# A masked prefix sum gathered at the midpoint: SyncE and TensorE loop over pairs of batches

## The chip, the core and the metric

The kernel runs on one core of one Trainium2 chip. The metric is the device time of one execution in microseconds (us), the median of several runs. The profile's times are in us from the start of the profiled span.

The engines that matter here: TensorE (PE in the profile; its weight loads are PEld, its sequencer PEq), VectorE (DVE), ScalarE (ACT), GpSimd (POOL) and SyncE (SP). Each runs its own list of instructions; they meet only at semaphores. SP and ACT also issue transfers, which 16 DMA engines carry out, and a transfer that has landed adds 16 to its semaphore.

## The reference

```
def reference(x, lengths, w):
    B, S, D = x.shape                      # 8, 8192, 512
    pos = np.arange(S)[None, :, None]
    mask = (pos < lengths[:, None, None]).astype(np.float32)
    masked = x * mask
    cs = np.cumsum(masked, axis=1)
    midpoints = (lengths // 2).clip(0)
    b_idx = np.arange(B)
    mid_features = cs[b_idx, midpoints, :]
    return np.matmul(mid_features[:, None, :], w).squeeze(1).astype(np.float32)
```

For each batch this is the sum of the first n = min(length // 2 + 1, length) rows of x, times w. Only those rows have to be read. The inputs are the same in every run; the eight values of n are 570, 2690, 256, 2057, 905, 3772, 3859 and 571. In blocks of 512 rows (1 MB) that is 1, 5, 0, 4, 1, 7, 7 and 1 whole blocks, 26 in all, and remainders of 58, 130, 256, 9, 393, 188, 275 and 59 rows.

## The kernel before

The sums are matrix products: a block of 512 rows lies as four rows in each of 128 partitions (G = 4), and TensorE multiplies it from the left by a matrix of 128 x 8 whose column b is one and whose other columns are zero (`sel`, shifted by b). The four rows of a partition go to four column groups of the array (`tile_position`), and all products of all batches are added up in one PSUM tile, `s_ps`. One matmul of the program is two matmul and two weight-load instructions in the profile, so a block is 8 of each.

The code is written out for all eight batches, and each batch has code for up to NB = 8 blocks, behind a branch for each block: `whole_blocks` (L107) goes on while n is at least 512 (k + 1).

SP (L118 to L182) first issues the load of the lengths, `lens1` (L120), which takes every other 32-bit word. `Counts` (L86) waits for it, loads the eight lengths into registers (L95), and works out n when a batch is first asked for (L101: three register operations, one fused instruction). Then come all blocks of all batches, in order (L135). Batch b writes to half b % 2 of `xt`, place k. Before it may, `wait_free` (L124) waits until TensorE has consumed what was there: `s_free[c]` counts the blocks of batch c that are done, and the newest earlier batch of the same half that has a block k is searched by branches (L127). Behind all blocks come the remainders of all batches (L147 to L178), each into a place of its own in `rem`: for each of 256, 128 and 64 one transfer if that bit of n is set (L152), and one for up to 64 last rows (L164). GpSimd clears the eight places of `rem` first, 14.1 us of work (L199). At the end SP issues half of the output (L182).

ACT issues the load of `w` (L187, 1 MB) and of a copy of the lengths for all partitions, `lens` (L188), at the start, and the other half of the output at the end.

VectorE makes `sel`, then the `mask` that says which of a remainder's places hold rows that count, in a chain of small steps (L210 is the helper that records each), among them `fold`, `cnt` and `cap`. Last it copies `s_ps`, `mf_ps` and `o_ps` out of PSUM, each when TensorE is done with it.

TensorE clears `s_ps` with eight products of zeros (L267), loads its own copy of the counts, goes through the blocks of all batches (L273 to L279; the matmul's line is that of the helper, L261), then waits for the mask and goes through the eight remainders (L282 to L286). Then it folds the four column groups into one and transposes in one product (L291), and multiplies by w (L298).

What sets the order of the work: SP's one list (all blocks, then all remainders), and TensorE's (the same). Everything else is beside it.

Of the kernel before, what the change touches and what calls it, by code (L numbers as in the profile page):

```python
# [8 lines left out]
I32 = mybir.dt.int32  # L9
ALU = mybir.AluOpType  # L10
ds = bass.ds
P = 128
# [3 lines left out]
def kernel(  # L16
# [22 lines left out]
    PARTS = [(256, 0, 2), (128, 1, 4), (64, 3, 8)]  # L39
    LAST = (7, 8)  # L40
    xf = x.rearrange("b s d -> (b s) d")
# [4 lines left out]
    def sb(name, shape, dt=F32):  # L46
        return ctx.enter_context(nc.sbuf_tensor(name, shape, dt))
# [4 lines left out]
    def sem(name):  # L52
        return tc.alloc_semaphore(name)

    xt = sb("xt", [P, 2, NB, G, D])
    rem = sb("rem", [P, B, G, D])
    wt = sb("wt", [P, KC, D])
    lens1 = sb("lens1", [1, B], I32)
# [8 lines left out]
    mask = sb("mask", [P, B * (G * B + 1)])  # L67
    sel = sb("sel", [P, 2 * B - 1])
# [11 lines left out]
    s_full = [[sem(f"full{b}_{k}") for k in range(NB)] for b in range(B)]  # L80
    s_rem = [sem(f"rem{b}") for b in range(B)]
    s_free = [sem(f"free{b}") for b in range(B)]
    s_w, s_len, s_len1, s_out = sem("w"), sem("len"), sem("len1"), sem("out")
    s_pool, s_dve, s_pe = sem("pool"), sem("dve"), sem("pe")

    class Counts:  # L86


        def __init__(self, eng):
            self.eng = eng  # L90
            self.regs = [eng.alloc_register(f"n_{eng.engine.name}_{b}") for b in range(B)]
            self.t = eng.alloc_register(f"t_{eng.engine.name}")
            self.known = 0
            eng.wait_ge(s_len1, 16)
            eng.load(self.regs, lens1[:])  # L95

        def __getitem__(self, b):
            while self.known <= b:

                n = self.regs[self.known]  # L100
                self.eng.reg_alu(self.t, n, 1, ALU.logical_shift_right)  # L101
                self.eng.reg_alu(self.t, self.t, 1, ALU.add)
                self.eng.reg_alu(n, self.t, n, ALU.min)
                self.known += 1
            return self.regs[b]

    def whole_blocks(eng, n, body, k=0):  # L107
        if k < NB:
            with eng.If_cmp(n, BLK * (k + 1), "IS_GE"):  # L109
                body(k)  # L110
                whole_blocks(eng, n, body, k + 1)

    POOL_REM = 1 + B
    DVE_SEL, DVE_MASK = 3, 28
# [3 lines left out]
    @block.sync  # L118
    def _(sp):
        sp.dma_start(out=lens1[:], in_=lens_words[:, ::2]).then_inc(s_len1, 16)  # L120
        ns = Counts(sp)
        t = ns.t

        def wait_free(b, k):  # L124

            if b >= 0:
                with sp.If_cmp(ns[b], BLK * (k + 1), "IS_GE"):  # L127
                    sp.wait_ge(s_free[b], k + 1)
                with sp.Else():
                    wait_free(b - 2, k)  # L130

        for b in range(B):
            def load_block(k):
                wait_free(b - 2, k)
                sp.dma_start(  # L135
                    out=xt[:, b % 2, k],
                    in_=x[b, k * BLK:(k + 1) * BLK].rearrange("(p g) d -> p g d", g=G),
                ).then_inc(s_full[b][k], 16)

            whole_blocks(sp, ns[b], load_block)  # L140

        def rows(b, first, count):
            return xf[ds(sp.snap(first) + b * S, count)]

        sp.wait_ge(s_pool, POOL_REM)
        base = sp.alloc_register("base")
        for b in range(B):  # L147
            for count, first, step in PARTS:
                sp.reg_alu(t, ns[b], count, ALU.bitwise_and)
                with sp.If_cmp(t, 1, "IS_GE"):  # L150
                    sp.reg_alu(base, ns[b], ~(2 * count - 1), ALU.bitwise_and)
                    sp.dma_start(  # L152
                        out=rem[first::step, b],
                        in_=rows(b, base, count).rearrange("(p g) d -> p g d", g=G),
                    ).then_inc(s_rem[b], 16)
                with sp.Else():
                    sp.sem_inc(s_rem[b], 16)
            sp.reg_alu(t, ns[b], 63, ALU.bitwise_and)
            sp.reg_alu(base, ns[b], ~63, ALU.bitwise_and)

            def load_last(lo, hi):

                if hi - lo == 1:
                    sp.dma_start(  # L164
                        out=rem[LAST[0]::LAST[1], b, :hi],
                        in_=rows(b, base, 16 * hi).rearrange("(g p) d -> p g d", p=16),
                    ).then_inc(s_rem[b], 16)
                    return
                mid = (lo + hi) // 2
                with sp.If_cmp(t, 16 * mid, "IS_GT"):  # L170
                    load_last(mid, hi)
                with sp.Else():
                    load_last(lo, mid)

            with sp.If_cmp(t, 1, "IS_GE"):
                load_last(0, 4)
            with sp.Else():
                sp.sem_inc(s_rem[b], 16)  # L178

        sp.wait_ge(s_dve, DVE_MASK + 3)  # L180
        for j in range(0, 4, 2):
            sp.dma_start(out=out[:, j * P:(j + 1) * P], in_=o_sb[32 * j:32 * j + B]).then_inc(s_out, 16)  # L182
        sp.wait_ge(s_out, 64)

    @block.scalar
    def _(act):
        act.dma_start(out=wt[:], in_=w.rearrange("(kc p) d -> p kc d", p=P)).then_inc(s_w, 16)  # L187
        act.dma_start(out=lens[:], in_=lens_words.to_broadcast((P, 2 * B))).then_inc(s_len, 16)  # L188
        act.wait_ge(s_dve, DVE_MASK + 3)
        for j in range(1, 4, 2):  # L190
            act.dma_start(out=out[:, j * P:(j + 1) * P], in_=o_sb[32 * j:32 * j + B]).then_inc(s_out, 16)

    @block.gpsimd
    def _(pool):
        pool.iota(pid[:], pattern=[[0, 1]], base=0, channel_multiplier=1)
        pool.iota(thr_i[:], pattern=[[128, G]], base=0, channel_multiplier=1)
        pool.iota(fold_i[:], pattern=[[-1, B]], base=128, channel_multiplier=1).then_inc(s_pool, 1)
        for b in range(B):
            pool.memset(rem[:, b], 0.0).then_inc(s_pool, 1)  # L199

    @block.vector
    def _(dve):
        done = 0

        def step(do, *args, **kw):

            nonlocal done
            if done:
                dve.wait_ge(s_dve, done)
            do(*args, **kw).then_inc(s_dve, 1)  # L210
            done += 1

        step(dve.memset, zero[:], 0.0)
        step(dve.memset, sel[:], 0.0)
        step(dve.memset, sel[:, B - 1:B], 1.0)
        assert done == DVE_SEL
        step(dve.memset, mask[:], 0.0)
# [7 lines left out]
        for value, first, every in [(c, f, e) for c, f, e in PARTS] + [(63, *LAST)]:  # L225
# [10 lines left out]
        step(dve.tensor_scalar, out=fold[:], in0=fold_i[:], scalar1=0, scalar2=None,  # L236
             op0=ALU.is_equal)
# [7 lines left out]
        step(dve.tensor_tensor,  # L245
             out=mask[:].rearrange("p (b q) -> p b q", b=B)[:, :, 0:G * B:B],
             in0=cap[:].unsqueeze(2).to_broadcast((P, B, G)),
             in1=thr[:].unsqueeze(1).to_broadcast((P, B, G)), op=ALU.is_gt)
        assert done == DVE_MASK
        dve.wait_ge(s_pe, 1)  # L250
        step(dve.tensor_copy, out=s_sb[:], in_=s_ps[:])
        dve.wait_ge(s_pe, 2)
        step(dve.tensor_copy, out=mf_sb[:].rearrange("p a b -> p (a b)"), in_=mf_ps[:, :KC * B])
        dve.wait_ge(s_pe, 3)
# [3 lines left out]
    def _(pe):  # L258
        def add(j, weights, rows):

            return pe.matmul(s_ps[32 * j:32 * j + weights.shape[-1]], lhsT=weights, rhs=rows,  # L261
                             start=False, stop=False, skip_group_check=True,
                             tile_position=(0, 32 * j))
# [6 lines left out]
        for b in range(B):  # L270
            one = sel[:, B - 1 - b:2 * B - 1 - b]

            def add_block(k):  # L273
                pe.wait_ge(s_full[b][k], 16)
                for j in range(G):
                    mm = add(j, one, xt[:, b % 2, k, j])
                mm.then_inc(s_free[b], 1)

            whole_blocks(pe, ns[b], add_block)  # L279

        pe.wait_ge(s_dve, DVE_MASK)
        for b in range(B):  # L282
            pe.wait_ge(s_rem[b], 16 * (len(PARTS) + 1))
            for j in range(G):
                at = (b * G + j) * B
                mm = add(j, mask[:, at:at + B], rem[:, b, j])  # L286
        mm.then_inc(s_pe, 1)
# [44 lines left out]
```

## Time and profile before

| | us |
|---|---|
| median of 3 runs (97.46 to 98.53) | 97.99 |
| the profiled execution | 98.02 |
| its span, first to last instruction | 96.2 |
| PE busy | 55.1 |
| POOL busy | 14.6 |
| DVE busy | 11.3 |

The span and the time of the execution differ by 1.8 us, which lie outside the first and last instruction. The profile's groups are sorted by cost; "idle before" is the time that the engine had nothing to do just before the group's instructions, and the arrow names what ended it. The granted TensorE clock was 0.75 on the mean. The DMA queues moved 31.39 MB in all, 326 GB/s over the span; between 9.5 and 69.5 us it is 416 to 428 GB/s in every stretch of 10 us.

### The profile page before, as it was taken

The numbers are of one execution on the slowest core, as the hardware profiler recorded it, in microseconds if no ns is written. First come the engines' busy times: TensorE is split into PE (matmuls) and PEld (weight loads), VectorE is DVE, ScalarE is ACT, GpSimd is POOL, SyncE is SP. The second block draws the span as 40 slices with busy tenths as digits, with TensorE's granted clock in tenths as the row PEclk, the third lists the DMA queues.
The fourth block names the chain that finished last, engine by engine and source line by source line (L and its number), as shares of the span: only waits on it lengthen the run. The fifth ranks groups of instructions, "written<-read, shape, count | busy, mean of one in ns | idle before, by whom it ended". The sixth has DMA issues, their size and how long they took to land.

```text
span 96.2 us, 1092 instructions
## 1 busy us (share of the span) xinstructions
PE 55.1 (57%) x320; PEld 7.1 (7%) x320; DVE 11.3 (12%) x31; POOL 14.6 (15%) x15
## 2 busy tenths in 40 slices
PE   1600077774672963649744475773476669996800
PEld 0000000000000100000000000000000011221600
DVE  3789910000000000000000000000000000002010
POOL 6999994000000000000000000000000000000000
PEclk9999999999555588555599955559755555999975
DMA  1835999999999999999999999999999999200000
GB/s 26 306 108 167 412 432 429 426 429 419 422 426 412 419 422 426 412 426 412 415 429 419 419 419 432 409 422 419 432 412 362 346 378 286 83 23 0 0 7 3
DMA packets 5275, 31.39 MB, mean 326 GB/s; under 512 B 832, under 2 KB 864, under 8 KB 1648
## 3 DMA queue, kind: packets, MB, share of 16 engines
q1 hardware_dynamic: 4560, 30.19, 77.6%
q10 hardware_dynamic: 704, 1.07, 3.5%
q8 instruction: 5, 0.08, 0.4%
q14 instruction: 6, 0.05, 0.1%
HBM read 31.24 MB, written 0.02 MB: 325 GB/s over the span
## 4 chain that ended last, share of the span: by engine, by line
DMA 61%; PE 15%; SPq 11%; issue 7%; DVE 1%
DMA xt<-in_x_dram 56%; PE s_ps L261 13%; SPq L135 7%; DMA lens<-in_lengths_dram 5%; SPq L127 1%; PE o_ps L298 1%; PE mf_ps L291 1%; SPq L109 1%; SPq L95 1%; DVE s_sb L210 1%; SPq L101 1%; DVE o_sb L210 0%; DVE mf_sb L210 0%; SPq L327 0%; SPq L44 0%
## 5 line engine op out<-in xcount | busy, mean ns | idle before, releaser
L261 PE MATMUL s_ps<-xt,sel 128*8 128x512 f32 x208 | 43.2, 927 | 33.2 <-DMA xt<-in_x_dram 29.1
L199 POOL MEMSET rem<- 128x2048 f32 x8 | 14.1, 1814 | 0.0
L210 DVE COPY s_sb<-s_ps 128x512 f32<-128x512 f32 x1 | 0.7, 692 | 75.6 <-PE s_ps L261 75.6
L261 PEld LDWEIGHTS s_ps<-xt,sel 128*8 128x8 f32 x208 | 3.3, 91 | 73.0 <-DMA xt<-in_x_dram 64.9
L261 PE MATMUL s_ps<-rem,mask 128*8 128x512 f32 x64 | 8.2, 667 | 0.0
L267 PE MATMUL s_ps<-zero 1*32 1x512 f32 x8 | 1.9, 1055 | 1.9 <-DVE sel L210 1.9
L261 PEld LDWEIGHTS s_ps<-rem,mask 128*8 128x8 f32 x64 | 1.8, 102 | 6.9 <-issue 6.3
L210 DVE TENSOR_SCALAR fold<-fold_i 128x8 f32<-128x8 int32 x1 | 1.7, 1732 | 0.0
L210 DVE TENSOR_SCALAR cap<-cnt 128x8 int32<-128x8 int32 x1 | 1.7, 1732 | 0.0
L210 DVE TENSOR_SCALAR cnt<-lens 128x8 int32<-128x8 int32 x1 | 1.7, 1664 | 0.1
L291 PE MATMUL mf_ps<-fold,s_sb 128*128 128x8 f32 x8 | 1.1, 259 | 0.8 <-DVE s_sb L210 0.8
L298 PE MATMUL o_ps<-wt,mf_sb 128*8 128x128 f32 x32 | 1.1, 273 | 0.3 <-DVE mf_sb L210 0.3
L291 PEld LDWEIGHTS mf_ps<-fold,s_sb 128*128 128x128 f32 x8 | 1.0, 191 | 1.8 <-DVE s_sb L210 1.8
L298 PEld LDWEIGHTS o_ps<-wt,mf_sb 128*8 128x8 f32 x32 | 0.8, 89 | 0.4 <-DVE mf_sb L210 0.4
L210 DVE TENSOR_SCALAR tmp<-tmp 128x1 int32<-128x1 int32 x5 | 0.8, 153 | 0.2
L210 DVE TENSOR_SCALAR fold_i<-fold_i 128x8 int32<-128x8 int32 x1 | 0.7, 686 | 0.0
L210 DVE CUSTOM_DVE_ANT_0 bits<-bits,tmp 128x2 uint16<-128x2 uint16 x4 | 0.6, 159 | 0.1
L210 DVE TENSOR_SCALAR tmp<-pid 128x1 int32<-128x1 int32 x4 | 0.6, 154 | 0.1
L210 DVE MEMSET zero<- 1x512 f32 x1 | 0.5, 485 | 1.1 <-SPq L44 1.1
L210 DVE TENSOR_SCALAR thr_i<-thr_i 128x4 int32<-128x4 int32 x1 | 0.5, 457 | 0.1
L210 DVE COPY o_sb<-o_ps 128x128 f32<-128x128 f32 x1 | 0.3, 291 | 1.2 <-PE o_ps L298 1.2
L267 PEld LDWEIGHTS s_ps<-zero 1*32 1x32 f32 x8 | 0.2, 132 | 1.9 <-DVE sel L210 1.9
(16 smaller groups left out, 2.3 us busy)
## 6 DMA issues: line engine op xcount, KB each, us to landing
xt<-in_x_dram SPq DMA_DIRECT2D x26, 1024.0 KB, 13.0
rem<-in_x_dram SPq DMA_DIRECT2D x3, 512.0 KB, 15.5
wt<-in_w_dram ACTq DMA_DIRECT2D x1, 1024.0 KB, 5.3
rem<-in_x_dram SPq DMA_DIRECT2D x3, 256.0 KB, 14.9
rem<-in_x_dram SPq DMA_DIRECT2D x3, 128.0 KB, 15.4
rem<-in_x_dram SPq DMA_DIRECT2D x3, 32.0 KB, 19.1
rem<-in_x_dram SPq DMA_DIRECT2D x1, 64.0 KB, 13.6
out_dram<-o_sb SPq DMA_DIRECT2D x2, 4.0 KB
```

What stands on the lines that cost most here:

```text
L95: eng.load(self.regs, lens1[:])
L101: self.eng.reg_alu(self.t, n, 1, ALU.logical_shift_right)
L109: with eng.If_cmp(n, BLK * (k + 1), "IS_GE"):
L127: with sp.If_cmp(ns[b], BLK * (k + 1), "IS_GE"):
L135: sp.dma_start(out=xt[:, b % 2, k], in_=x[b, k * BLK:(k + 1) * BLK].rearrange("(p g) d -> p g d", g=G),).then_inc(s_full[b][k], 16)
L199: pool.memset(rem[:, b], 0.0).then_inc(s_pool, 1)
L210: do(*args, **kw).then_inc(s_dve, 1)
L261: return pe.matmul(s_ps[32 * j:32 * j + weights.shape[-1]], lhsT=weights, rhs=rows, start=False, stop=False, skip_group_check=True, tile_p ...
L267: pe.matmul(s_ps[32 * j:32 * j + 32], lhsT=zero[:, :32], rhs=zero[:], start=True, stop=False, skip_group_check=True, tile_position=(0, 32 ...
L291: mm = pe.matmul(mf_ps[:, kc * B:(kc + 1) * B], lhsT=s_sb[:, kc * P:(kc + 1) * P], rhs=fold[:], start=True, stop=True)
L298: mm = pe.matmul(o_ps[32 * j:32 * j + B, :P], lhsT=mf_sb[:, kc], rhs=wt[:, kc, j * P:(j + 1) * P], start=(kc == 0), stop=(kc == KC - 1), t ...
```

## The change

SP and TensorE now run a loop of four passes, each over a pair of batches, in which the batches of a pair have fixed places (q = 0 and 1):

- Semaphores belong to places instead of batches: one for each of the 16 places of `xt` full and free, two each for the remainders' places full and free, two for `cur`. A waiter takes: it waits for the value and lowers the semaphore by it (`take`), so that the next pass finds it as the first did. GpSimd opens the 16 places of `xt` at the start, by raising each free semaphore by one.
- SP works through a batch's blocks and then through the same batch's remainder, where all blocks stood ahead of all remainders. The row of x is in a register (`base`), so the block loads have an address from a register. `rem` has two places; before it loads into one, SP takes `s_rfree[q]`, which GpSimd gives for the first use, and VectorE for later ones once TensorE is done with the batch two before.
- `lens1` is loaded as one run of 16 words, and `Counts` loads 16 registers, keeps every other one, and works out all eight n at once. At the end of a pass `next_pair` moves the registers down by two.
- SP issues the load of `w` behind that of `lens1`; ACT waits for `lens1` before it issues `lens`.
- `sel` and `mask` become one `table` with 40 columns for each batch: the 8 columns for whole blocks and the 32 for the remainder. VectorE copies the columns of a batch into `cur[:, q]`, and TensorE takes `s_cur[q]` before it starts the batch. `fold` is now made behind the mask.
- TensorE goes through a batch's blocks and then its remainder, and raises `s_pe` after each batch.

```
+    def take(eng, s, n):
+        eng.wait_ge(s, n).then_inc(s, -n)
...
-            self.regs = [eng.alloc_register(f"n_{eng.engine.name}_{b}") for b in range(B)]
...
+            regs = [eng.alloc_register(f"n_{eng.engine.name}_{i}") for i in range(2 * B)]
+            self.t = t = eng.alloc_register(f"t_{eng.engine.name}")
             eng.wait_ge(s_len1, 16)
-            eng.load(self.regs, lens1[:])
+            eng.load(regs, lens1[:])
+            self.regs = regs[::2]
+            for n in self.regs:
+                eng.reg_alu(t, n, 1, ALU.logical_shift_right)
+                eng.reg_alu(t, t, 1, ALU.add)
+                eng.reg_alu(n, t, n, ALU.min)
...
+        def next_pair(self):
+            for to, of in zip(self.regs, self.regs[2:]):
+                self.eng.reg_mov(to, of)
...
     def _(sp):
-        sp.dma_start(out=lens1[:], in_=lens_words[:, ::2]).then_inc(s_len1, 16)
+        sp.dma_start(out=lens1[:], in_=lens_words).then_inc(s_len1, 16)
+        sp.dma_start(out=wt[:], in_=w.rearrange("(kc p) d -> p kc d", p=P)).then_inc(s_w, 16)
         ns = Counts(sp)
...
+        with sp.Fori(0, B // 2):
+            for q in range(2):
+                n = ns[q]
+                def load_block(k):
+                    take(sp, s_free[q][k], 1)
+                    sp.dma_start(
+                        out=xt[:, q, k],
+                        in_=rows(k * BLK, BLK).rearrange("(p g) d -> p g d", g=G),
+                    ).then_inc(s_full[q][k], 16)
+                whole_blocks(sp, n, load_block)
+                take(sp, s_rfree[q], 1)
+                for count, first, step in PARTS:
+                    sp.reg_alu(t, n, count, ALU.bitwise_and)
+                    with sp.If_cmp(t, 1, "IS_GE"):
...
+                sp.reg_alu(base, base, S, ALU.add)
+            ns.next_pair()
...
     def _(act):
-        act.dma_start(out=wt[:], in_=w.rearrange("(kc p) d -> p kc d", p=P)).then_inc(s_w, 16)
+        act.wait_ge(s_len1, 16)
         act.dma_start(out=lens[:], in_=lens_words.to_broadcast((P, 2 * B))).then_inc(s_len, 16)
...
     def _(pool):
+        for q in range(2):
+            for k in range(NB):
+                pool.sem_inc(s_free[q][k], 1)
...
-        for b in range(B):
-            pool.memset(rem[:, b], 0.0).then_inc(s_pool, 1)
+        for q in range(2):
+            pool.memset(rem[:, q], 0.0).then_inc(s_rfree[q], 1)
...
+        for b in range(B):
+            if b == 0:
+                dve.wait_ge(s_dve, done)
+            if b >= 2:
+                dve.wait_ge(s_pe, b - 1)
+                dve.sem_inc(s_rfree[b % 2], 1)
+            dve.tensor_copy(out=cur[:, b % 2], in_=table[:, b * WT:(b + 1) * WT]).then_inc(s_cur[b % 2], 1)
...
+        with pe.Fori(0, B // 2):
+            for q in range(2):
+                take(pe, s_cur[q], 1)
+                def add_block(k):
+                    take(pe, s_full[q][k], 16)
+                    for j in range(G):
+                        mm = add(j, cur[:, q, :B], xt[:, q, k, j])
+                    mm.then_inc(s_free[q][k], 1)
+                whole_blocks(pe, ns[q], add_block)
+                take(pe, s_rem[q], 16 * (len(PARTS) + 1))
                 for j in range(G):
-                    mm = add(j, one, xt[:, b % 2, k, j])
...
+                    mm = add(j, cur[:, q, B + j * B:2 * B + j * B], rem[:, q, j])
+                mm.then_inc(s_pe, 1)
+            ns.next_pair()
```

More of the change, by code (lines that the diff above doesn't have):

```diff
@@ L40 @@
     LAST = (7, 8)
+    WT = B + G * B
     xf = x.rearrange("b s d -> (b s) d")
@@ L66 @@
     thr = sb("thr", [P, G], I32)
-    mask = sb("mask", [P, B * (G * B + 1)])
-    sel = sb("sel", [P, 2 * B - 1])
+    table = sb("table", [P, B * (WT + 1)])
+    cur = sb("cur", [P, 2, WT])
     zero = sb("zero", [1, D])
@@ L132, in _ @@
-        for b in range(B):
[L133 to L178, printed above, removed]
@@ L213, in _ @@
         step(dve.memset, zero[:], 0.0)
-        step(dve.memset, sel[:], 0.0)
-        step(dve.memset, sel[:, B - 1:B], 1.0)
         assert done == DVE_SEL
-        step(dve.memset, mask[:], 0.0)
+        step(dve.memset, table[:], 0.0)
+        tab = table[:].rearrange("p (b q) -> p b q", b=B)
+        step(dve.memset, tab[:, :, 0:1], 1.0)
         step(dve.memset, o_ps[:, :P], 0.0)
@@ L224, in _ @@
         step(dve.memset, bits[:], 0)
-        for value, first, every in [(c, f, e) for c, f, e in PARTS] + [(63, *LAST)]:
+        for value, first, every in PARTS + [(63, *LAST)]:
             step(dve.tensor_scalar, out=tmp[:], in0=pid[:], scalar1=every - 1, scalar2=None,
@@ L259, in add @@
         def add(j, weights, rows):
-            return pe.matmul(s_ps[32 * j:32 * j + weights.shape[-1]], lhsT=weights, rhs=rows,
+            return pe.matmul(s_ps[32 * j:32 * j + B], lhsT=weights, rhs=rows,
                              start=False, stop=False, skip_group_check=True,
```

87 lines of the change are left out of this document (45 added, 42 removed).

## The prediction

> **What bounds the kernel now.** I read the page first (slices, queues, chain, groups, issues), then TensorE's timeline and the queue view of short stretches, then the chain at the start and SP's own waits. Span, DMA slices, the largest group and the largest issue of the page:
>
> ```profile
> span 96.2 us, 1092 instructions
> DMA  1835999999999999999999999999999999200000
> L261 PE MATMUL s_ps<-xt,sel 128*8 128x512 f32 x208 | 43.2, 927 | 33.2 <-DMA xt<-in_x_dram 29.1
> xt<-in_x_dram SPq DMA_DIRECT2D x26, 1024.0 KB, 13.0
> ```
>
> The DMA engines are full from the fourth slice to the 34th, and TensorE's largest wait is for xt: the kernel moves 26 blocks and the remainder rows, and TensorE follows. TensorE's timeline shows the pace (columns: start, us, what, idle before and why):
>
> ```profile
> 11.93 1.90 PE L261 MATMUL s_ps<-xt,sel 128*8 128x512 f32 x8 [8.07 <-DMA xt<-in_x_dram]
> 14.41 1.90 PE L261 MATMUL s_ps<-xt,sel 128*8 128x512 f32 x8 [0.59 <-DMA xt<-in_x_dram]
> ...
> 19.38 1.71 PE L261 MATMUL s_ps<-xt,sel 128*8 128x512 f32 x8 [0.59 <-DMA xt<-in_x_dram]
> 22.54 1.04 PE L261 MATMUL s_ps<-xt,sel 128*8 128x512 f32 x8 [1.45 <-DMA xt<-in_x_dram]
> ...
> 63.72 1.73 PE L261 MATMUL s_ps<-xt,sel 128*8 128x512 f32 x8 [0.59 <-DMA xt<-in_x_dram]
> 66.92 1.05 PE L261 MATMUL s_ps<-xt,sel 128*8 128x512 f32 x8 [1.48 <-DMA xt<-in_x_dram]
> ...
> 71.90 1.90 PE L261 MATMUL s_ps<-xt,sel 128*8 128x512 f32 x8 [0.60 <-DMA xt<-in_x_dram]
> 75.49 1.89 PE L261 MATMUL s_ps<-xt,sel 128*8 128x512 f32 x8 [1.69 <-DMA xt<-in_x_dram]
> 78.31 1.90 PE L261 MATMUL s_ps<-xt,sel 128*8 128x512 f32 x8 [0.93 <-DMA xt<-in_x_dram]
> ...
> 79.98 0.16 PEld L261 LDWEIGHTS s_ps<-rem,mask 128*8 128x8 f32 x4 [0.70 <-issue]
> ...
> 86.00 0.35 PEld L261 LDWEIGHTS s_ps<-rem,mask 128*8 128x8 f32 x8 [0.51 <-DMA rem<-in_x_dram]
> 88.22 0.69 DVE L210 COPY s_sb<-s_ps 128x512 f32<-128x512 f32 x1 [75.64 <-PE s_ps L261]
> ```
>
> A block lands every 2.49 us (11.93 to 14.41, rounded up), but some steps are longer: 19.38 to 22.54 is 0.67 over, 63.72 to 66.92 0.71, 71.90 to 75.49 1.10. The 25 steps from 11.93 to 78.31 take 66.4 us where 25 x 2.49 is 62.2. The queue view explains some of it. Its rows here (queue: packets, MB, share) are for the stretch 7 to 80 us (two rows) and for 71.5 to 72.2; the stretches 20.0 to 20.6 and 63.3 to 64.0 also hold one packet of q14:
>
> ```profile
> q8 instruction: 4, 0.07, 0.4%
> q14 instruction: 5, 0.04, 0.1%
> ...
> q14 instruction: 1, 0.01, 2.9%
> ```
>
> These are engines fetching code, in pieces of about 8 KB (q14) and 16 KB (q8), and each of the three long steps has one just ahead. A block counts as landed when its slowest DMA engine is done, so I read the long steps as fetches that hold up one engine. The three make 2.48 us: 0.5 for each of five fetches if the other two cost nothing, 0.83 if only these three are charged; I take 0.6. That q14's are SyncE's is an inference: it runs the long code in that time. TensorE turns to the remainders at 79, but still waits for one at 86.00: what ends the kernel is the last landing, plus 2.2 us to the copy at 88.22 and a fixed end. TensorE's 8 us of remainders are work done while it waits.
>
> **The change, part by part.** The sum is made against the profiled execution: 98.02 us, span 96.2, beside a median of 97.99. The start and the queue ends:
>
> ```profile
> 0.96 5.05 DMA lens<-in_lengths_dram
> 6.03 0.73 SPq L95
> 6.80 0.14 SPq L101
> 7.09 0.38 SPq L135
> 0.91 0.44 ACTq L187 DMA_DIRECT2D wt<-in_w_dram  x1
> 91.75 0.72 SPq L182 DMA_DIRECT2D out_dram<-o_sb  x2
> SPq _compat.py:109 <- DMA out_dram<-o_sb: 1.2, 1, 1.2
> 47.50 4.28 SPq L135 DMA_DIRECT2D xt<-in_x_dram  x2
> 53.88 0.70 SPq L164 DMA_DIRECT2D rem<-in_x_dram  x1
> L152 SPq DMA_DIRECT2D rem<-in_x_dram x6: 476/496/540, 55.5 to 70.4; - x6
> SPq L127 <- PE s_ps L261: 19.0, 8, 5.2
> ```
>
> 1. *The lengths and w.* Now lens1 lands at 6.01, 5.05 after its issue, with the 1 MB of wt issued 0.05 us before it from another queue. In the changed kernel lens1 is alone and wt follows it on SP. A small DMA on empty queues, the output, was waited for 1.2 us after its issue ended (91.75 + 0.72 to about 93.7). By that lens1 lands at 0.96 + 0.84 (its issue row ends at 1.80) + 1.2, some 3.1. The ends are 3.0 and 6.0; I take 3.1, because wt ahead is the only difference I see. [...] wt's own issue, 0.44 on SP, lies inside the wait for lens1, and its bytes move before xt's as now.
> 2. *Counts.* The load has 16 registers in place of 8 at 0.73: between 0.73 and 1.47, I take 1.1. All eight lengths are worked out before the first load: 8 x 0.12 (L101's three operations take 0.12 to 0.14) = 0.95 in place of 0.14. Loop entry, branch, take and address: 0.35, which is the 0.15 that lies between L101's end (6.94) and the issue (7.09) for one branch now, and an estimate of 0.2 for the rest. First xt issue: 3.1 + 1.1 + 0.95 + 0.35 = 5.5, in place of 7.09. With 11.93 - 7.09 = 4.84 to its landing, and 0.1 more because the address is now in a register, it lands at 10.45: **-1.4**.
> 3. *Register addresses.* 26 issues go from 0.33 to about 0.50 (L152). That is 4.4 us of SP's queue, covered by the 19.0 us in which SP waits for TensorE. Without that cover it would still be 0.85 an issue against 2.49 a transfer.
> 4. *Remainders behind their own batch.* b0 has one block, and its remainder stands before b1's first block on SP: from 51.78 (47.50 + 4.28) to 54.58, that is 2.8 us. b1's block is issued at 6.1 + 2.8 = 8.9 and lands no earlier than 13.8, where the queue alone would land it at 10.45 + 0.3 + 2.49 = 13.3: **+0.4** (0 to 1). Bytes stay the same. The places in rem are double instead of eightfold, so each remainder from b2 on waits until TensorE is done two batches back; POOL clears 2 places instead of 8. Its 16 new semaphore steps, which open the places of xt, stand ahead of its iotas; VectorE, which waits for those, has 1.6 us to spare (step 5: idle from 6.6 to 8.2).
> 5. *cur.* TensorE's first matmul now waits for the whole mask and a copy. The lengths for the mask are issued by ACT after lens1 and take up to 5 us (lens1's time now), to 8.2:
>
> ```profile
> 6.66 1.73 DVE L210 TENSOR_SCALAR fold<-fold_i 128x8 f32<-128x8 int32 x1
> 8.49 1.66 DVE L210 TENSOR_SCALAR cnt<-lens 128x8 int32<-128x8 int32 x1
> 12.36 0.22 DVE L210 TENSOR_TENSOR mask<-cap,thr 128x32 f32<-128x32 int32 x1
> L109 PEldq COMPARE_BRANCH x34: 64/64/3596, 7.1 to 78.3; - x34
> ```
>
> From cnt's start to the mask's end is 4.1 (8.49 to 12.58), fold's 1.73 now comes behind, the copy is some 0.2: 8.2 + 4.1 + 1.7 + 0.2 = 14.2, against 11.93. TensorE starts 1.5 blocks late and catches up, since a block costs it 1.04 to 1.90 of 2.49. SP's remainder of b2 waits for b0 to be done, 14.2 + 1.67 (78.31 to 79.98) + 1.04 (eight matmuls at 22.54) = 16.9; what is queued by then (6.4 MB) lands until 10.45 + 5.4 x 2.49 = 23.9. Seven us of cover: nothing.
> 6. *Loop code.* SP's program now runs 4 passes over a body of a quarter of the code, with simpler waits: one and a half to two of the pieces of which straight code fetched five. No row shows a jump backwards. Ends: one fetch in all (everything stays) to seven or more (both pieces in each of three returns, and one behind). I take four, one a pass: one fewer than now, **-0.6**. TensorE's fetches (q8) should mostly go; what they add to the slowest engine I put at **-0.4** (0 to -0.7, the long step at 19.38 as its measure).
> 7. *The end.* b7's block and its 128 KB remainder (0.3 us apart) now land last: 1.67 + 1.04 (as in step 5) - 0.3 = 2.4 after the last landing, in place of 2.2: **+0.2**. The eight remainders leave the end, but they were covered there.
>
> Sum: -1.4 + 0.4 - 0.6 - 0.4 + 0.2 = -1.8, so 98.0 - 1.8 = **96.2 us**.
>
> **The rivals.**
> *All code stays.* One fetch instead of five: -2.4 in place of -0.6 in step 6, 94.4 us. For it: the body is a quarter of the code. Against: five fetches in straight code show that pieces are brought in ahead, and nothing shows one kept.
> *Both pieces are fetched again at each return.* Seven fetches: +1.2 in place of -0.6, and TensorE's -0.4 is gone: 98.4 us. For it: the fetches come in order of the code, with no sign that an earlier piece stays.
> *The queue runs dry (the slower side).* A branch to code that is not there can hold its engine for long: on TensorE one of 34 took 3.596 us, the others 0.064 at the median. SP may be held for one such time in a pass or, with both pieces, two. The tight place is the pass to b4: b3's remainder must wait for TensorE's end of b1 (its last block lands at 13.8 + 4 x 2.49 = 23.8, and it and the remainder take some 2.5: 26.3), takes up to 2.8 (step 4), and b4's block is issued at about 29.5; 10.9 MB lie ahead, landing until 10.45 + 9.9 x 2.49 = 35.1, so an issue before 35.1 + 2.49 - 4.95 = 32.6 costs nothing. One hold (33.1) costs 0.5; two (36.7) cost 4.1, less the 0.7 by which the slow engine is behind then anyway: 96.2 + 3.4 = 99.6 us. From one hold on it begins; two decide. [...]
> *lens1 is late for another reason than wt.* It lands at 6.0 as now: 2.9 later, 99.1 us. For it: nothing in the trace says what held it. Against it: the output's 1.2 us.
>
> **How the numbers follow.** 96.2 (35 in 100, own range 95.2 to 97.4); all code stays, 94.4 (23); seven fetches, 98.4 (20); queue dry, 99.6 (13); lens1 late, 99.1 (9). The range goes from 93.9 (the first rival with half a microsecond to spare) to 99.6. One per cent, about what a measurement of this kernel can tell, is 1.0 us. Faster (under 97.0): 0.23 and four fifths of 0.35, 0.51. Same: 0.07 of the 0.35, 0.17 of the 0.20 and 0.04 of the lens1 case, 0.28. Slower: the rest, 0.21.
>
> **What would show it.** Right: SP's first xt issue near 5.5 and the first block's matmul near 14.2; the last landing about 2 us earlier; fewer instruction packets; long steps fewer than four. Wrong: lens1 past 5 us; more than five q14 fetches before the last landing; a slice under 9 in the DMA row between 30 and 40 us; TensorE waiting for cur or s_full with the queue empty.

## The result, and the profile after

The changed kernel takes 94.9 us (median of 4, 94.61 to 97.24); the kernel before, on the same chip, 97.85 (97.46 to 98.53). The ratio is 0.9681, 95% interval 0.9607 to 0.9756. The profiled execution took 94.75 us with a span of 92.8, against 98.02 and 96.2. The prediction was 96.2, with a range of 93.9 to 99.6 that holds the result; its own range for the likeliest case, 95.2 to 97.4, doesn't. Medians here are over all executions of a kernel; ratios leave the disturbed ones out, so that the two need not agree to the last digit.

The page of the changed kernel, its span, DMA slices and instruction queues:

```profile
span 92.8 us, 1217 instructions
...
DMA  0799799999999999999999999999999999700000
GB/s 0 220 303 388 215 420 417 431 431 424 413 424 406 431 413 410 418 409 427 417 427 420 424 413 418 338 410 424 420 420 424 420 420 373 292 17 0 0 7 4
...
q8 instruction: 1, 0.02, 0.1%
q14 instruction: 2, 0.02, 0.1%
```

Three things are new: the stream of transfers starts a slice earlier, it has a hole in the fifth slice (215 GB/s, about 9.3 to 11.6 us), and of q14's and q8's eleven packets (six and five) three are left. In the page of before, the rate falls at the end of the stream:

```profile
GB/s 26 306 108 167 412 432 429 426 429 419 422 426 412 419 422 426 412 426 412 415 429 419 419 419 432 409 422 419 432 412 362 346 378 286 83 23 0 0 7 3
```

From the 31st slice on (362, 346, 378, 286, 83), where the last block and then the remainders were landing, the rate was lower. In the changed kernel the remainders lie among the blocks, and the rate holds until the 33rd slice, but for the 26th (338), in which the remainders of b5 land. So the new order made them no cheaper: the packets of blocks and remainders together take 74.5 us of each DMA engine's time on the mean before, and 74.7 in the changed kernel.

The timeline of the changed kernel at the start (start, us, what); the two L147 rows are SyncE's first blocks, b0's and then b1's:

```profile
0.97 0.34 SPq L130 DMA_DIRECT2D lens<-in_lengths_dram  x1
...
1.37 0.44 SPq L131 DMA_DIRECT2D wt<-in_w_dram  x1
2.19 0.39 ACTq L197 DMA_DIRECT2D lens<-in_lengths_dram  x1
2.54 3.57 POOL L211 MEMSET rem<- 128x2048 f32 x2
4.88 0.39 SPq L147 DMA_DIRECT2D xt<-in_x_dram  x1
...
8.95 1.12 SPq L147 DMA_DIRECT2D xt<-in_x_dram  x2
```

ScalarE's issue at 2.19 marks lens1's landing, which came at 6.0 before. SyncE's first block goes out at 4.88 in place of 7.09, and between 5.27 and 8.95 SyncE is in the branches of b0's remainder and issues it. TensorE's timeline, with VectorE's copy of the sums behind it:

```profile
10.14 1.90 PE L279 MATMUL s_ps<-xt,cur 128*8 128x512 f32 x8 [6.55 <-PEq L93]
...
14.46 1.24 PE L279 MATMUL s_ps<-xt,cur 128*8 128x512 f32 x8 [0.72 <-PEq L93]
...
19.41 1.04 PE L279 MATMUL s_ps<-xt,cur 128*8 128x512 f32 x8 [1.42 <-PEq L93]
21.91 1.89 PE L279 MATMUL s_ps<-xt,cur 128*8 128x512 f32 x8 [1.45 <-PEq L93]
...
68.50 1.89 PE L279 MATMUL s_ps<-xt,cur 128*8 128x512 f32 x8 [0.60 <-PEq L93]
70.97 1.64 PE L279 MATMUL s_ps<-xt,cur 128*8 128x512 f32 x8 [0.58 <-PEq L93]
...
82.85 1.29 PE L279 MATMUL s_ps<-xt,cur 128*8 128x512 f32 x8 [0.64 <-PEq L93]
...
85.06 0.69 DVE L222 COPY s_sb<-s_ps 128x512 f32<-128x512 f32 x1 [22.35 <-PE s_ps L279]
```

PEq L93 is the lowering of a semaphore in `take`: it now stands between TensorE and the transfer that it waits for, so a wait for a transfer is shown under that line. The copy comes at 85.06 in place of 88.22, 3.2 us earlier, and stands 2.2 behind the last block's release at 82.85, as it stood 2.2 behind the last remainder's (86.00) before. So nothing was won between the last landing and the copy: 3.2 of the 3.4 us by which the span is shorter are an earlier last landing, and the rest lies behind the output. The hole is in the two steps at the top: 10.14 to 14.46 holds one block (2.49) and b0's 58 rows (0.3), and is 1.5 us longer than these.

### The profile page after: what moved, and what is told of

Read it like the earlier page. It is cut to its first block, busy times and chain, and to the rows that moved or that the text cites. A ratio compares the mean times of both kernels' runs of the same rounds, so it can differ in the third digit from the quotient of the medians.

```text
span 92.8 us, 1217 instructions
## 1 busy us (share of the span) xinstructions
PE 53.3 (57%) x320; PEld 8.3 (9%) x320; DVE 8.8 (10%) x38; POOL 4.0 (4%) x9
## 5 line engine op out<-in xcount | busy, mean ns | idle before, releaser
L279 PE MATMUL s_ps<-xt,cur 128*8 128x512 f32 x208 | 38.9, 817 | 31.8 <-PEq L93 31.8
L279 PE MATMUL s_ps<-rem,cur 128*8 128x512 f32 x64 | 12.0, 826 | 0.3 <-PEq L93 0.3
L279 PEld LDWEIGHTS s_ps<-xt,cur 128*8 128x8 f32 x208 | 4.3, 89 | 65.9 <-issue 65.8
L267 DVE COPY cur<-table 128x40 f32<-128x40 f32 x8 | 1.4, 184 | 52.6 <-PE s_ps L279 52.6
L211 POOL MEMSET rem<- 128x2048 f32 x2 | 3.6, 1816 | 0.0
L279 PEld LDWEIGHTS s_ps<-rem,cur 128*8 128x8 f32 x64 | 2.1, 111 | 9.9 <-issue 9.8
L222 DVE TENSOR_SCALAR thr_i<-thr_i 128x4 int32<-128x4 int32 x1 | 1.7, 1734 | 0.2 <-POOL fold_i L209 0.2
## 6 DMA issues: line engine op xcount, KB each, us to landing
xt<-in_x_dram SPq DMA_DIRECT2D x26, 1024.0 KB, 12.8
```

The costliest lines, as they stand in the source:

```text
L211: pool.memset(rem[:, q], 0.0).then_inc(s_rfree[q], 1)
L267: dve.tensor_copy(out=cur[:, b % 2], in_=table[:, b * WT:(b + 1) * WT]).then_inc(s_cur[b % 2], 1)
L279: return pe.matmul(s_ps[32 * j:32 * j + B], lhsT=weights, rhs=rows, start=False, stop=False, skip_group_check=True, tile_position=(0, 32 * j))
```

## Experiments

Two theories stood against each other at first. A: the gain is the code that is no longer fetched. B: it is the new order of the transfers, and the fetches don't matter. With the fifth run the start came in, as theory S. Each experiment was compared with the kernel before on its own chip (97.9 to 98.2 us there).

**The changed kernel as a mark, and its loops written out.** The changed kernel again, then SyncE's loop alone written out, TensorE's alone, and both:

```
-        with sp.Fori(0, B // 2):
+        for _ in range(B // 2):
...
-        with pe.Fori(0, B // 2):
+        for _ in range(B // 2):
```

> The changed kernel as it is, as the mark for the other three. Both theories: about 94.8 us, one code fetch of SyncE's (q14) and one of TensorE's (q8) while the blocks stream. Theory A (code): the stream of transfers is shorter than before because the looped code is fetched twice in all instead of some nine times. Theory B (order): it is shorter because the remainders lie among the blocks instead of behind them, and the fetches don't matter.

> SyncE's loop written out in four passes, with the same order of transfers, the same semaphores and the same places; TensorE keeps its loop. Theory A: four to five q14 fetches more in the stream, at 0.5 to 0.8 us on the slowest DMA engine each, so 2 to 3 us slower than the changed kernel, about 97 us. Theory B: order unchanged, so 94.8 us, within half a microsecond of the changed kernel.

> TensorE's loop written out in four passes, SyncE keeps its loop. Theory A: three to five q8 fetches of 16 KB instead of one; TensorE is held some 3.6 us once or twice, which the queue covers, and the slowest DMA engine is up to 0.7 us later: 94.8 to 95.6 us. Theory B: 94.8 us.

> Both loops written out, all else as in the changed kernel: what is left of the change without loops. Theory A: 97 to 98 us, as slow as the kernel before or nearly so, with nine or ten fetches. Theory B: 94.8 us.

The mark took 95.12 us, ratio 0.9669 (0.9602 to 0.9736); SyncE written out 95.96, 0.9783 (0.9742 to 0.9825); TensorE written out 94.99, 0.9651 (0.9591 to 0.971); both 95.72, 0.9763 (0.9721 to 0.9805). SyncE's loop is worth 0.8 us by the medians and 1.1 by the ratios, TensorE's nothing that can be told. Theory A asked for about 97 us with SyncE written out and 97 to 98 with both, theory B for 94.8 in either: both missed. The fetches count, but most of the gain is there without loops.

The page with SyncE written out has q14 six times, that with TensorE written out q8 five times:

```profile
q14 instruction: 6, 0.05, 0.1%
```

```profile
q8 instruction: 5, 0.08, 0.3%
```

So q14's fetches are SyncE's and q8's TensorE's, as the prediction inferred. What a fetch costs is seen in TensorE's timeline with SyncE written out:

```profile
13.86 1.24 PE L279 MATMUL s_ps<-xt,cur 128*8 128x512 f32 x8 [0.24 <-PEq L93]
...
18.84 1.04 PE L279 MATMUL s_ps<-xt,cur 128*8 128x512 f32 x8 [1.44 <-PEq L93]
21.73 1.89 PE L279 MATMUL s_ps<-xt,cur 128*8 128x512 f32 x8 [1.85 <-PEq L93]
...
69.19 1.90 PE L279 MATMUL s_ps<-xt,cur 128*8 128x512 f32 x8 [1.44 <-PEq L93]
72.39 1.90 PE L279 MATMUL s_ps<-xt,cur 128*8 128x512 f32 x8 [1.31 <-PEq L93]
...
84.15 1.29 PE L279 MATMUL s_ps<-xt,cur 128*8 128x512 f32 x8 [1.39 <-PEq L93]
```

The steps from 18.84 and 69.19 are those that were shown of the changed kernel from 19.41 and 68.50 (2.50 and 2.47 there); here they are 2.89 and 3.20, and each has one of q14's packets in it (at 19.5 and 70.4 us). From b1's first block to b7's it is 70.29 in place of 68.39: 1.9 us for the five fetches of SyncE between them, 0.4 each. The trace also has the 16 landings of each block, read here as one for each of the 16 DMA engines. At b7's block, the slowest engine against the median one, and the last landing of all, in the profiled executions:

```
                       median engine   slowest behind it   last landing
changed (the mark)          80.5             1.4               82.3
SyncE written out           80.4             3.6               84.3
TensorE written out         80.9             1.8               82.9
both written out            80.7             3.6               84.5
```

The stream as a whole is not slower with straight code; its slowest engine falls behind (3.6 us in place of 1.4), and TensorE waits for that one: in the kernel before, 23 of the 26 blocks start 0.04 us behind the last of their 16 landings, and in the first profile of the changed kernel those that it waited for start 0.13 to 0.14 behind it. The 2.0 us between the first two last landings are more than the 0.8 of the medians, for two reasons. The mark's profiled execution (93.97) is the fastest of its six; against the first profile of the changed kernel, with its last landing at 83.0, it is 1.3 (1.9 less the 0.6 by which b1's first block came earlier). And with SyncE written out the span ends 3.7 us behind the issue of the output, in the mark 4.2; why isn't shown.

**The start alone.** The kernel before, with the load of the lengths as one run, `w` behind it on SyncE, and sixteen registers. Each n is still worked out when its batch is first asked for, so that the first block goes out at 3.68, against 4.88 in the changed kernel:

```
-        sp.dma_start(out=lens1[:], in_=lens_words[:, ::2]).then_inc(s_len1, 16)
+        sp.dma_start(out=lens1[:], in_=lens_words).then_inc(s_len1, 16)
+        sp.dma_start(out=wt[:], in_=w.rearrange("(kc p) d -> p kc d", p=P)).then_inc(s_w, 16)
...
-        act.dma_start(out=wt[:], in_=w.rearrange("(kc p) d -> p kc d", p=P)).then_inc(s_w, 16)
+        act.wait_ge(s_len1, 16)
```

> The kernel before with the start of the changed one alone: the lengths loaded as one run of 16 words into 16 registers, w issued by SyncE behind them, ACT's load of lens behind lens1. All blocks, then all remainders, code written out, as before. Theory S (the start): lens1 lands near 2.2, the first block near 9.7 in place of 11.9, and without a hole in the stream behind it all of that is gained: about 96 us. Theory O (the order of the transfers makes the gain, an earlier start is lost later on): 97.5 to 98 us.

95.92 us (95.7 to 96.63), ratio 0.9778 (0.9734 to 0.9822): the start alone gives 2.2 us, two thirds of the gain. The busy times by stretch (the last two columns are DMA share and GB/s), of the kernel before and of this one, and this one's first issue of blocks:

```profile
6.00:8.00 2.00, 0.00 (x0) 0.00 (x0) 1.97 (x2) 2.00 (x2) 1.00 0.00 0
```

```profile
6.00:8.00 2.00, 0.00 (x0) 0.00 (x0) 1.97 (x2) 2.00 (x2) 1.00 0.70 211
```

```profile
3.68 2.84 SPq L137 DMA_DIRECT2D xt<-in_x_dram  x5
```

Before, the DMA engines did nothing from 6 to 8 us: `w` had landed, and the first block was issued only at 7.09. Now they are busy for 0.70 of this stretch. Theory S has the larger part, theory A the rest. This kernel and the changed one with both loops written out are alike (0.9778 and 0.9763): the new order of the transfers, `cur` and the places add up to nothing that can be told. Why the hole near 10 us doesn't show in that comparison is seen from 5.5 to 11.5 us, in this kernel and in the one with both loops written out:

```profile
5.50:11.50 6.00, 0.34 (x4) 0.12 (x8) 5.72 (x7) 6.00 (x4) 1.00 0.85 328
```

```profile
5.50:11.50 6.00, 1.52 (x8) 0.31 (x12) 2.88 (x18) 0.60 (x1) 1.00 0.83 283
```

The engines stand idle for about the same time in both (a share of 0.85 and 0.83; 0.54 before): one has a hole behind its first block, the other a gap between `w` and its first block (a share of 0.49 from 5.5 to 7.0, against 0.88), although it issues that block earlier. What makes this gap isn't shown.

**What held lens1.** The changed kernel, once with `w` issued by ScalarE at the very start as before, and once with lens1 as every other word again but `w` behind it:

```
-        sp.dma_start(out=wt[:], in_=w.rearrange("(kc p) d -> p kc d", p=P)).then_inc(s_w, 16)
...
+        act.dma_start(out=wt[:], in_=w.rearrange("(kc p) d -> p kc d", p=P)).then_inc(s_w, 16)
```

```
-        sp.dma_start(out=lens1[:], in_=lens_words).then_inc(s_len1, 16)
+        sp.dma_start(out=lens1[:], in_=lens_words[:, ::2]).then_inc(s_len1, 16)
```

> The changed kernel with the 1 MB of w issued by ACT at the start, as before, so that it stands ahead of or beside lens1. If wt is what held lens1: lens1 lands near 6, the first block near 13.5, 3 us later than in the changed kernel, about 98 us. If it was the form of the old lens1 transfer (every other word): lens1 lands near 2.2 all the same, 94.8 to 95.2 us.

> The changed kernel with lens1 loaded as before, every other word into 8 registers; w stays behind it on SyncE's queue. If wt ahead was what held it: lens1 lands between 2.2 and 3, the register load is 0.4 us shorter, 94.5 to 95 us. If the form held it: lens1 lands near 5 to 6, 97 to 98 us.

95.21 us (0.9655, 0.9592 to 0.9717) and 95.48 (0.9678, 0.9625 to 0.9732): neither undoes the gain. ScalarE's issue of `lens`, for which it waits for lens1, in the timeline of the first, and SyncE's of lens1 and ScalarE's of `lens` in that of the second:

```profile
2.18 0.37 ACTq L197 DMA_DIRECT2D lens<-in_lengths_dram  x1
```

```profile
0.97 0.85 SPq L130 DMA_DIRECT2D lens<-in_lengths_dram  x1
...
2.96 0.39 ACTq L197 DMA_DIRECT2D lens<-in_lengths_dram  x1
```

With `w` ahead and the words in one run, lens1 has landed by 2.18. With every other word and `w` behind, the issue takes 0.85 and lens1 has landed by 2.96. Only both together, as in the kernel before, made it 6.0. There the trace has nine landings of lens1: one at 2.19 and eight from 5.85 to 6.01, amid those of `w` (5.66 to 6.23).

**The hole: blocks of both batches first.** SyncE issues the blocks of both batches of a pair and then both remainders, and TensorE goes in the same order (SyncE's half):

```
                 whole_blocks(sp, n, load_block)
+                sp.reg_alu(base, base, S, ALU.add)
+            for q in range(2):
+                n = ns[q]
                 take(sp, s_rfree[q], 1)
```

> The changed kernel with another order in each pass, on SyncE and on TensorE: the blocks of both batches of the pair, then the remainders of both. The first remainder's branches then no longer stand between b0's only block and b1's first. If SyncE's time there makes the hole in the stream near 10 us, the hole goes and about 1.2 us with it: 93.5 to 94 us. If the hole has another cause, or TensorE falls behind in the new order: 94.8 us or more.

94.74 us (93.58 to 95.75), ratio 0.9536 (0.9476 to 0.9596). TensorE's timeline at the start and the end:

```profile
9.96 1.89 PE L284 MATMUL s_ps<-xt,cur 128*8 128x512 f32 x8 [6.37 <-PEq L93]
12.44 1.90 PE L284 MATMUL s_ps<-xt,cur 128*8 128x512 f32 x8 [0.58 <-PEq L93]
...
79.87 1.90 PE L284 MATMUL s_ps<-xt,cur 128*8 128x512 f32 x8 [0.78 <-PEq L93]
...
81.53 3.36 PE L284 MATMUL s_ps<-rem,cur 128*8 128x512 f32 x16
```

The second block comes 2.48 behind the first, so the hole is gone, and the last landing is at 81.6 in place of 82.3 to 83.0. Part of it goes again at the end, where two remainders (3.36 us) stand behind the last block. The 1.5 us by which TensorE waited too long for its second block were not all lost to the DMA engines: from 5.5 to 11.5 us their busy share is 1.00 here and 0.85 to 0.92 in the three profiles of the changed kernel, which is 0.5 to 0.9 us, and at the last transfer, b7's remainder, the median engine lands at 80.4 in place of 80.9 to 81.5. The median says 0.2 to 0.4 us won, the ratio 1.2: the size isn't settled.

**The same order with both loops written out.** The edits of the two kernels above together.

> The pair order (blocks of both batches of a pair, then both remainders) with both loops written out: the fetches of the kernel before, no hole near 10 us. If the hole costs 1.2 us where the fetches are the same, 94.3 to 94.7 us, against 95.7 with both loops written out and the changed kernel's order. If the hole is filled again behind the slowest DMA engine, 95.7 us as there.

97.25 us (96.33 to 98.23), ratio 0.9892 (0.9825 to 0.9958): 2.5 us slower than the same order in loops, and slower than the written-out code with the hole (95.72). At b7's block the median engine is at 78.2 in both, but the slowest is 4.6 behind it in place of 1.5; at the last transfer, b7's remainder, the median engine is at 80.6, against 80.4 in loops, and the slowest 3.9 behind it in place of 1.2. The expectation took the gains of the two edits for independent, and they are not. With both loops written out the slowest engine is 3.6 behind at b7's block in the changed order and 4.6 in this one, and the last landing is at 84.5 in both: what was won by closing the hole is gone again. That is measured; why the fetches hold up the slowest engine by more here is not. The rest lies behind the last landing: TensorE then has two remainders to do in place of one, and VectorE's copy comes at 87.64 in place of 86.35.

**The hole: remainders from another queue.** The changed kernel, with the remainders issued by ScalarE in a loop of its own; TensorE's order stays:

```
     def _(act):
         act.wait_ge(s_len1, 16)
         act.dma_start(out=lens[:], in_=lens_words.to_broadcast((P, 2 * B))).then_inc(s_len, 16)
+        ns = Counts(act)
...
+        with act.Fori(0, B // 2):
+            for q in range(2):
+                n = ns[q]
+                take(act, s_rfree[q], 1)
+                for count, first, step in PARTS:
+                    act.reg_alu(t, n, count, ALU.bitwise_and)
+                    with act.If_cmp(t, 1, "IS_GE"):
...
```

> The changed kernel with the remainders issued by ACT, in a loop of its own, so that SyncE issues blocks alone; TensorE's order is the changed kernel's. If SyncE's time for b0's remainder is what makes the hole near 10 us, the hole goes as in the pair order, and TensorE has less to do behind the last landing than there: 93.3 to 94 us. If two queues get in each other's way, or ACT's own code fetches weigh: 95 us or more.

93.61 us (93.04 to 104.49), ratio 0.9532 (0.948 to 0.9584). The profile is of the execution that took 104.49 us, far above the others, so the rows below are those of a second run of this kernel, beside the changed one:

> The kernel after the change, unchanged, as the mark for the run beside it: 94.5 to 95.2 us, first block of TensorE near 10.1, a slice of the stream near 10 us well under the others, last landing 82.3 to 83.1.

> The kernel after the change with the remainders issued by ScalarE in a loop of its own, while SyncE issues whole blocks alone. Theory (the hole near 10 us is SyncE's, held up between the first batch's blocks and the second's by the remainder's branches): no hole, the second batch's first block lands near 12.8 instead of 14.3, the last landing near 81.5 and the time 93.0 to 93.8. Rival (the queue is never short of work for long, and what is lost near 10 us is won back): last landing 82.5 to 83, 94.6 to 95.2.

The changed kernel 94.77 us (0.9655, 0.9595 to 0.9715); remainders from ScalarE 93.22 (93.06 to 94.03), ratio 0.9517 (0.9467 to 0.9567). This is faster than both kernels, than the changed one by 1.5 us of the medians and by 0.7 in the two profiled executions (93.75 against 94.41). The stretch of the hole, in the first profile of the changed kernel and in this one:

```profile
9.30:11.60 2.30, 1.46 (x8) 0.32 (x12) 0.00 (x0) 0.00 (x0) 1.00 0.76 216
```

```profile
9.30:11.60 2.30, 1.67 (x8) 0.15 (x8) 0.00 (x0) 0.00 (x0) 1.00 0.99 412
```

2.3 us at 216 in place of 412 GB/s is 1.1 us of transfers; by the busy share, 0.76 and 0.99, the engines were idle for 0.5 us of it. The second batch's first block landed at 13.3, where 12.8 was expected, and at 13.9 in the changed kernel beside it. This kernel's end, in TensorE's timeline:

```profile
79.35 1.89 PE L293 MATMUL s_ps<-xt,cur 128*8 128x512 f32 x8 [0.59 <-PEq L93]
...
81.00 1.66 PE L293 MATMUL s_ps<-rem,cur 128*8 128x512 f32 x8
...
82.48 1.03 PE L293 MATMUL s_ps<-xt,cur 128*8 128x512 f32 x8
...
83.34 1.03 PE L293 MATMUL s_ps<-rem,cur 128*8 128x512 f32 x8
```

The three groups at the end have no wait in front of them: from 79.35 on TensorE, no longer the DMA, sets the end. Against the changed kernel's profile beside it, the last landing is 1.0 us earlier (81.7 against 82.6), but VectorE's copy only 0.2 (84.45 against 84.64). SyncE's issue of the output, there and here:

```profile
88.17 0.71 SPq L191 DMA_DIRECT2D out_dram<-o_sb  x2
```

```profile
87.99 0.71 SPq L158 DMA_DIRECT2D out_dram<-o_sb  x2
```

The spans end at 92.4 and 91.7, 4.2 and 3.7 behind these issues. So of the 0.7 us between the two profiles 0.2 are won up to the output, and 0.5 lie behind it, where why isn't shown. That this kernel is faster is measured; how much of that is the hole is not settled.

## Why the prediction was right, and where not

Faster was right, and 96.2 was 1.3 us too slow. The measured sum is close to -2.2 for the start, -0.9 for SyncE's loop, nothing for TensorE's and nothing net for the order: -3.1, where the prediction had -1.8. The direction came from mechanisms that the runs bear out, an earlier start and fewer fetches; that 94.9 lies so near the 94.4 of the rival "all code stays" is luck, since that rival had -1.4 for the start and -2.8 for all fetches.

*Steps 1 and 2, the start: -1.4 predicted, -2.2 measured with the start alone.* The mechanism was right, the term mis-sized. lens1 was put at 3.1 and landed by 2.19: its issue took 0.34, where the 0.84 of the strided load was charged, and 0.88 to landing, where 1.2 was taken from the output. SyncE's first issue came at 4.88 in place of 5.5. More than that, the first block's landing was the wrong measure for what the start is worth: with the start alone the first block was waited for until 11.16 (0.8 earlier) while the last x8 group of a block moved from 78.31 to 76.04 (2.3 earlier). The median engine landed the first block 1.8 us earlier (9.9 against 11.7) and the last one 1.7 (72.3 against 74.0). The slowest engine was 1.3 behind it at the first block, where it had been 0.2 behind, but 3.7 at the last, where it had been 4.3.

```profile
11.16 1.89 PE L263 MATMUL s_ps<-xt,sel 128*8 128x512 f32 x8 [7.31 <-DMA xt<-in_x_dram]
...
76.04 1.90 PE L263 MATMUL s_ps<-xt,sel 128*8 128x512 f32 x8 [0.90 <-DMA xt<-in_x_dram]
```

*"wt ahead is the only difference I see"* failed. The load's form is another, and mending either alone would have been enough. The rival that hung on it (lens1 late for another reason, 99.1) fell all the same.

*Step 4, the remainder ahead of b1's block: +0.4 predicted* (its own two figures, 13.8 and 13.3, are 0.5 apart). The issue was put at 8.9 and came at 8.95. But the queue alone would have landed that block at 10.14 + 0.3 + 2.49 = 12.93, and from its issue it took 5.5 in place of 4.95: 14.46, 1.5 late. Taking the cause away moved the last landing 1.0 us earlier and made the medians 1.5 shorter (93.22 against 94.77), of which the hole is a part that isn't settled. The term was too small; by the last landing it should have been two to three times as large. That the order of the change still came out at nothing net has its reason at the same place: with the blocks first, the engines lose as much time between `w` and the first block (the shares of 0.85 and 0.83 above).

*Step 5, cur: no cost predicted, none found, by other numbers.* TensorE's first block was put at 14.2 and came at 10.14, when the block had landed (10.0), because VectorE's chain was short and `cur` was ready before it:

```profile
2.63 1.73 DVE L222 TENSOR_SCALAR thr_i<-thr_i 128x4 int32<-128x4 int32 x1 [0.16 <-POOL fold_i L209]
...
7.47 0.17 DVE L222 TENSOR_SCALAR cnt<-lens 128x8 int32<-128x8 int32 x1
...
8.74 0.28 DVE L267 COPY cur<-table 128x40 f32<-128x40 f32 x2
```

The step that failed is the sum of 4.1, from `cnt`'s start to the mask's end, and `fold`'s 1.73: most of the 1.66 and 1.73 of before was not work but waiting. The rows of before that show it (fold and cnt were shown; their ends are 8.39 and 10.15):

```profile
1.28 14.13 POOL L199 MEMSET rem<- 128x2048 f32 x8
```

```profile
3.27 0.15 DVE L210 TENSOR_SCALAR tmp<-pid 128x1 int32<-128x1 int32 x1
...
5.93 0.69 DVE L210 TENSOR_SCALAR fold_i<-fold_i 128x8 int32<-128x8 int32 x1
...
10.19 1.73 DVE L210 TENSOR_SCALAR cap<-cnt 128x8 int32<-128x8 int32 x1
```

GpSimd's eight clears take 1.77 each on the mean (14.13 / 8), so they end at 6.58, 8.35, 10.11 and 11.88; VectorE's four slow instructions end at 6.62, 8.39, 10.15 and 11.92, each 0.04 behind one. In the changed kernel the clears are over at 6.11, cnt takes 0.17, and the one instruction that still meets a clear, `thr_i`, ends at 4.36, some 0.03 behind the end of the first (2.54 + 3.57 / 2). By these ends the slow instructions waited for a clear; what they wait for in it isn't shown.

*Step 6, the code: -1.0 predicted, about -0.9 measured, by another mechanism.* The likeliest case had four of SyncE's fetches in the stream at 0.6, one a pass. That step failed: the profile has one, near 9.3 us, in the first pass. The first rival, all code stays, is what happened, and that its sum for the code (-2.8) is so far from the measured one is the price of a fetch. Two rows speak against the other rivals, that of the branch at the loop's end (three returns and the exit) and that of SyncE's waits at `take`:

```profile
L141 SPq COMPARE_BRANCH  x4: 34/45/50, 16.1 to 65.2; - x4
```

```profile
SPq L93 <- SPq L93: 9.9, 5, 3.6
```

The branch back takes 0.05 us at most, and SyncE's five waits, 9.9 us in all, are for places of `xt` and `rem` that are not yet free. The price per fetch was 0.4 in the changed order, not 0.6, and TensorE's term was nothing in place of -0.4: with three more of its fetches in the stream (a fourth came behind it, at 83.9) the slowest engine was 1.8 behind in place of 1.4, and the time stayed where it was. The two rivals that had each return pay (98.4 and 99.6) fell, since no return was slow, and with them the slower side: the three returns and the exit lie between 16.1 and 65.2 us, where q14 has no packet. That a branch to code that is not there can hold its engine rested on one row, the 3.596 us of TensorE before: this branch stands from 38.20 to 41.80, with a packet of q8 in it (39.29, 1.02 long). The other four of q8's packets before went with no branch of TensorE over 0.35 us, and in the changed kernel none took more than that.

*Steps 3 and 7.* The addresses from registers cost nothing that can be seen: an issue of a block takes 0.336 us at the median, against 0.330 before. At the end 2.4 was forecast from the last landing to the copy; from the last block's release it is 2.2, as it was from the last remainder's before.

The chances came out on the right side, but the rival that was true had only 23 in 100: "nothing shows one kept" was no evidence, since straight code never returns to a piece and so cannot show whether one is kept.

## What to carry to other kernels

Code that is written out for every case can be paid for in the DMA stream: here the slowest DMA engine was 3.6 us behind the median one with five more fetches of SyncE's code in the stream, TensorE waited for that engine, and with a loop, whose stream has one such fetch, it was 1.4 behind, with returns of 0.05 us. At the start of a stream, count what the issuing engine executes between its first transfer and its second (here 3.7 us, from 5.27 to 8.95), since nothing is queued yet to cover it; of the two cures tried here, a second issuing engine has the shorter median (93.22 us against 94.74), with ratios of 0.9517 and 0.9536 that lie within each other's intervals. Where one instruction takes ten times what its like takes elsewhere (`cap` 1.73 us before, 0.17 in the changed kernel), look at whose instruction ends just before it does, before its duration goes into a sum.

## What the runs showed of the hardware that was not expected

- A load of eight words of 4 bytes, every other one, issued 0.05 us after a load of 1 MB on another queue, landed 5.05 us after its issue; as one run of sixteen words it landed 1.2 us after its issue with the same load ahead (2.18 against 0.97), and every other word with that load behind took 2.0 (2.96 against 0.97).
- VectorE's tensor_scalar over 8 integers in each partition took up to 1.73 us beside a clear by GpSimd and 0.17 without one, while one over a single integer in each took 0.15 beside it (the row at 3.27).
- A fetch of some 8 KB of code went with a delay of the slowest of the 16 DMA engines by 0.4 to 0.7 us (the two steps above), in a stream whose median engine shows nothing of it. The one fetch of q8 that is left in the changed kernel, near 28 us, went with a rise of the slowest engine's lag from 0.6 to 1.6 us; three more of them in the stream, with TensorE written out, added 0.4 together. Of SyncE's five fetches in its written-out code, the one at 32.1 went with no rise of the lag (1.4 before and behind it). Why some cost and others don't was not found.
